# Six of eight output chunks of the down projection: 320 + 320 token columns in place of 384 + 256

## The chip, the cores and the metric

The kernel runs on one core of one Trainium2 chip. The metric is the device time of one execution in microseconds (us); lower is better. Before the change three executions took 981.87, 982.79 and 984.15 us, so the median is 982.79 us.

The engines are named as in the profile: PE is the tensor engine's matrix multiplication, PEld its weight loading, DVE the vector engine, ACT the scalar engine, POOL GpSimd, SP the queue that issues the transfers. Instructions of one engine start in the order in which they were issued to it.

## The reference, cut to what matters

One layer of a diffusion backbone over 512 latent and 128 context tokens, 640 tokens in all, model width 1024. The change touches the last matrix product of the layer, the down projection of the gated feed-forward part, and the two elementwise steps behind it:

```
f_gate, f_val = jnp.split(up, 2, axis=-1)            # up: 640 tokens x 5632
f = (jax.nn.silu(f_gate) * f_val) @ prm["w_ffn_down"]  # (640 x 2816) @ (2816 x 1024)
x = x + g2 * rms_norm(f, prm["norm_ffn_post"])
```

`rms_norm` divides by the root of the mean square over the 1024 channels. Everything is float32 at the edges.

## The kernel before

Activations lie with channels on the 128 partitions and the 640 tokens along the free axis (`T = 640`). A float32 product is made of three products of rounded parts: weights and activations are each split into a high part (rounded to the PE's faster 32-bit format, fp32r) and a low remainder, and `mm3` adds high times high, high times low and low times high in one accumulator in PSUM. A weight block is 128 x 128, and each of the three products of a block is applied to all 640 tokens. One matmul writes at most one PSUM bank of 512 float32 columns, so 640 tokens need two matmuls. They are cut as `HC = ((0, 384), (384, 640))`: a matmul over 384 columns and then one over 256 columns, both with the same weights. Each matmul instruction is preceded by its own weight load, also the second one of a pair.

The cut at 384 has a second use: at several places the two column ranges are worked on one after the other as "halves" 0 and 1, so that elementwise work on one half runs beside matmuls on the other. There a half is a stream of matmuls of one width only.

An accumulator is a PSUM tile of 1024 columns, two banks (`psum`, called `ps` in the profile). `HALF`, inside the kernel function, has the place of each half: 384 columns from column 128 to the bank's end at 512, and 256 columns from 512. The 640 results thus lie next to each other over the border of the banks, and `view` gives them as one range, `t[:, 128:768]`.

The down projection (`down_mm`, `down_out`) makes 8 output chunks of 128 channels, `m` from 0 to 7. Each needs `NF = 22` weight blocks, that is 22 x 3 = 66 pairs of matmuls.

- Chunk 0 uses two single-bank tiles (`zero_at`, called `pq` in the profile) with 384 and 256 columns. It is interleaved with chunk 1: both run over blocks 0 to 15 first, and then over blocks 16 to 21.
- Chunks 1 to 6 use `ps` tiles and pass `half = None`: both column ranges, a pair for each weight.
- Chunk 7 is worked in halves: all 66 matmuls of 384 columns, then the 66 of 256 columns, among which stand the column sums for the norm of half 0.

When a chunk is finished `down_out` reads it from PSUM with ACT: the squares of all 640 columns (L1412, added up by POOL on L1414), then a copy scaled by a per-channel factor, in two parts because latent and context tokens have different factors (L1418). The next chunk takes another of three `ps` tiles meanwhile. Weights come by DMA in units of 8 blocks, and ACT (L311) and POOL (L313) split them into high (`wh`) and low (`wl`) parts ahead of their use.

The order of all instructions on each engine is written out in a table of numbers (`ORDER`); it counts instructions and knows nothing of their widths. In the profile every matmul of `mm3` has line L415. A similar helper on L1259 serves the first part of the up projection.

Of the kernel before, what the change touches and what calls it, by code (L numbers as in the profile page):

```python
# [17 lines left out]
T = L + C  # L18
HT = T // 2
HC = ((0, 384), (384, T))  # L20
NCH = T // P
KD = D // P
NPAIR = 8
# [6 lines left out]
NF = DFF // P  # L30
# [153 lines left out]
def hybrid_layer_kernel(ctx: ExitStack, tc: tile.TileContext, xT, ct, prm, cst, wrest, wdt, idhl_d, wada1, wada2, win,  # L184
# [20 lines left out]
    def nm(s):  # L205
        uid[0] += 1
        return f"{s}_{uid[0]}"


    def slot(tag, dt=F32, shape=(P, T)):  # L210
        if tag in ("H8", "T8"):
            return sb.tile([P, T + 64], dt, tag=tag, name=nm(tag))[:, 48:48 + shape[1]]
        return sb.tile(list(shape), dt, tag=tag, name=nm(tag))
# [4 lines left out]
    def psq(i):  # L218
        return ps.tile([P, 512], F32, tag=f"Q{i}", name=nm(f"pq{i}"))

    def view(t):
        return t[:, 128:128 + T]

    def prm_col(name, i=0, n=1):
        a = _COLS[name][0] + i
        return prms[:, a:a + n]
# [5 lines left out]
    for k in range(KD):  # L232
        t = slot(f"T{k}")
# [58 lines left out]
    def get_unit(i):  # L292
        fetch(i + AHEAD)
        return ready.pop(i)
# [43 lines left out]
    for p in range(NPAIR):  # L338
# [4 lines left out]
        last = p == NPAIR - 1  # L343
# [54 lines left out]
    def split_act(hi_tag, lo_tag, src, lo_eng):  # L398
        hi = slot(hi_tag, F32R)
        hi_ins[0] = ac.activation(hi, src, AF.Copy)  # L400
        lo = slot(lo_tag, F32R)
        split_ins[0] = lo_eng.tensor_tensor(lo, src, hi.bitcast(F32), SUB)
        return hi, lo

    last_mm = [None]
    HALF = ((128, *HC[0]), (512, *HC[1]))

    def mm3(pt, hi, lo, j, xh, xl, first, last, halves=(0, 1), places=None):
        w1 = hi[:, j * P:(j + 1) * P]
        w2 = lo[:, j * P:(j + 1) * P]  # L410
        for i, (w, x) in enumerate(((w1, xl), (w1, xh), (w2, xh)) if first else ((w1, xh), (w1, xl), (w2, xh))):
            for h in halves:
                o, c0, c1 = HALF[h]
                out = places[h] if places else pt[:, o:o + c1 - c0]
                last_mm[0] = te.matmul(out, w, x[:, c0:c1], start=first and i == 0, stop=last and i == 2)  # L415

# [108 lines left out]
    for s in range(4):  # L525
# [6 lines left out]
        for k in (k0, k0 + 1):  # L532
# [3 lines left out]
            hi, lo = split_act(f"H{k}", f"H{8 + k}", xs_[k], ve)  # L536
# [16 lines left out]
    def proj(n):  # L553
        (u,) = unit_of[n]
        hi, lo = get_unit(u)
        pt = psum(flip[0] % 2)
        flip[0] += 1
        for k in range(KD):
            mm3(pt, hi, lo, k, h_hi[k], h_lo[k], k == 0, k == KD - 1)
        return pt  # L560

    def conv3_silu(pt, i, out):
        v = view(pt)
        w = lambda j: prm_col("ssd_w", 3 * i + j)
        ac.activation(out, v, AF.Identity, bias=prm_col("ssd_b", i), scale=w(1))
        for c0, c1 in ((0, L), (L, T)):
            ve.scalar_tensor_tensor(out[:, c0 + 1:c1], v[:, c0:c1 - 1], w(0), out[:, c0 + 1:c1], MUL, ADD)
        for c0, c1 in ((0, L), (L, T)):
            ve.scalar_tensor_tensor(out[:, c0:c1 - 1], v[:, c0 + 1:c1], w(2), out[:, c0:c1 - 1], MUL, ADD)
        if i < NPAIR:  # L570

            tmp = sm.tile([P, T], F32, tag="tanh", name=nm("tanh"), bufs=1)
            ac.activation(tmp, out, AF.Tanh)
            ve.scalar_tensor_tensor(out, tmp, 1.0, out, ADD, MUL)
        else:
            ac.activation(out, out, AF.Silu)
# [7 lines left out]
    def chunked(t):  # L584
        return t.rearrange("p (c t) -> p c t", c=NCH)

# [9 lines left out]
    def dtprep():  # L596
# [5 lines left out]
        pd = psq(0)  # L602
        for c in range(NCH):
            te.matmul(pd[:, c * 32:(c + 1) * 32], raw[:, c * P:(c + 1) * P], ids, start=True, stop=True)
        W = NCH * 32
        scr = slot("T9")
        a, n, e, w = (scr[:, i * W:(i + 1) * W] for i in range(4))
        by = lambda t: t.rearrange("p (c h) -> p c h", c=NCH)
        ve.tensor_tensor(by(a), by(pd[:, 0:W]), prm_col("dt_bias", 0, 32).unsqueeze(1).to_broadcast([P, NCH, 32]), ADD)
        ve.scalar_tensor_tensor(n, a, -1.0, a, MUL, MAX)  # L610
        ac.activation(e, n, AF.Exp, scale=-1.0)

        DT = slot("T12")[:, 0:W].rearrange("p (c h) -> p c h", c=NCH)
        ve.tensor_scalar(n, e, 2.0, None, ADD)
# [235 lines left out]
    def gate(p, pg):  # L850
        for (o0, o1), (c0, c1) in UCOLS:
            ac.activation(ub[p % 3][:, o0:o1], view(pg)[:, c0:c1], AF.Tanh, scale=0.5)

    def gated(p, pa):
        u = ub[p % 3]
        for (o0, o1), (c0, c1) in UCOLS:
            ve.scalar_tensor_tensor(u[:, o0:o1], u[:, o0:o1], 1.0, view(pa)[:, c0:c1], ADD, MUL)
# [69 lines left out]
    for it in seq:  # L927
        if it[0] == "proj":
            n = it[1]
            pt = proj(n)  # L930
# [6 lines left out]
            elif n[0] == "B":  # L937
                g = int(n[1:])
                bT[g] = slot("M2")
                conv3_silu(pt, 8 + g, bT[g])  # L940
            elif n[0] == "C":
                g = int(n[1:])
# [58 lines left out]
    def ahead_parts():  # L1001
        for m in range(KD):
            w = get_unit(unit_of["ahead", m])
            pt = psum(2 if m in (5, 7) else 0)
            for k in range(NA):
                mm3(pt, *w, k, *mix[k], k == 0, k == NA - 1)
            o = ahead_sb[m] = slot(ASLOT[m])
            ac.activation(o, view(pt), AF.Copy)
# [29 lines left out]
    def next_ps():  # L1038
        rot[0] += 1
        return psum(rot[0] % 3)  # L1040

    BOTH = (0, 1)
    RANGES = (((0, *HC[0]),), ((0, HC[1][0], L), (1, L, T)))

    def cols_of(halves):
        return slice(HC[halves[0]][0], HC[halves[-1]][1])

    def ranges_of(halves):
        return ((0, 0, L), (1, L, T)) if len(halves) == 2 else RANGES[halves[0]]
# [49 lines left out]
    def xr_fetch():  # L1099
        for k in range(KD):  # L1100
            t = slot(f"T{8 + k}")
            sy.dma_start(t[:, slice(*HC[0])], xT[:, k, slice(*HC[0])])
            xr[0].append(t[:, slice(*HC[0])])

# [28 lines left out]
    class Mid:  # L1133
        def __init__(self, half):
            self.half, (self.c0, self.c1) = half, HC[half]
            self.n = self.c1 - self.c0
            self.t = {}
# [70 lines left out]
    for half in range(2):  # L1208
        for m in range(OUT_FULL, KD):
            pt = next_ps()  # L1210
# [32 lines left out]
    f_hl = [None] * NF  # L1243
    f_raw = [None] * NF
    for i in range(KD // 2):
        t = sb.tile([P, 2, HC[1][1] - HC[1][0]], F32, tag=f"H{i}", name=nm("xr"))
# [70 lines left out]
    for i in (0, 3, 4, 1, 2):  # L1317
        if i >= 3:
            pt = psq((i + 1) % 2)
# [22 lines left out]
    for i in range(HEAD, 2 * NF):  # L1342
        q, half = ups[i]
        w = get_unit(unit_of["up", i])
        pt = next_ps()
# [48 lines left out]
    def down_mm(m, half, pt, ks):  # L1394
        halves = BOTH if half is None else (half,)
        for k in ks:
            g = k // 8
            if k % 8 == 0 and not half:
                down_w[g] = get_unit(unit_of["down", m, g])
            mm3(pt, *down_w[g], k % 8, *f_hl[k], k == 0, k == NF - 1, halves, zero_at if m == 0 else None)  # L1400

    def down_out(m, half, pt):
        halves = BOTH if half is None else (half,)
        if mg[m] is None:
            mg[m] = slot(mtags[m])
        cc = cols_of(halves)
        v = zero_at[half] if m == 0 else view(pt)[:, cc]
        if m == 0:
            ac.activation(msq[:, cc], v, AF.Square)
        else:  # L1410
            sq = sq_last[0] if half else slot("AT" if m % 2 else "HL")
            ac.activation(sq[:, cc], v, AF.Square)  # L1412
            if half is None:
                gp.tensor_tensor(msq[:, cc], msq[:, cc], sq[:, cc], ADD)  # L1414
            else:
                sq_last[half] = sq
        for c, c0, c1 in ranges_of(halves):
            ac.activation(mg[m][:, c0:c1], v[:, c0 - cc.start:c1 - cc.start], AF.Copy, scale=gg2[:, m, c:c + 1])  # L1418

    down_w = {}  # L1420
# [30 lines left out]
    zero_at = [psq(h)[:, 0:HC[h][1] - HC[h][0]] for h in range(2)]  # L1451
    down_ps = [None, next_ps()]
    for ks in (range(0, 16), range(16, NF)):
        for m in range(2):
            down_mm(m, None, down_ps[m], ks)
            if ks[-1] == NF - 1:
                for half in (BOTH if m == 0 else (None,)):
                    down_out(m, half, down_ps[m])
    for m in range(2, KD - 1):
        pt = next_ps()  # L1460
        down_mm(m, None, pt, range(NF))
        down_out(m, None, pt)

    m = KD - 1
    pt = next_ps()
    down_mm(m, 0, pt, range(NF))
    down_out(m, 0, pt)
    pt = next_ps()
    k1, k2 = 3, 9
# [127 lines left out]
```

## Time and profile before

| | |
|---|---|
| median of the three timed executions | 982.79 us |
| the profiled execution, first to last instruction (its span) | 979.4 us |
| matmuls and weight loads recorded | 7623 each |
| six chunks with pairs in one `ps` tile each (m = 1 to 6) | within about 807 to 946.7 us of the span |
| mean granted tensor clock | 0.996 of full speed |

The profiled execution's own time is told as its span alone; the median of the timed executions is 3.4 us above that span. This is what lies around the first and the last instruction.

A row of the timeline gives the start of a group of like instructions in us from the span's start, the time from there to the end of the last of them, the engine, the line, output and inputs, and how many there are. Matmuls overlap in these records: the next one starts well before the record of the last one ends. What a stream of matmuls costs is therefore read from one start to the next and not from the length of a record.

A row "A <- B: us, times, longest" of the waits says how long engine and line A stood idle until B released it.

### The profile page before, as it was taken

The page shows a single profiled execution, that of the slowest core. Times are in us where ns is not written, and L with a number is a line of the kernel's source. Part 1 is how long each engine was busy: PE and PEld are TensorE (multiplying, and loading weights), DVE is VectorE, ACT ScalarE, POOL GpSimd, SP SyncE. Part 2 cuts the span into 40 slices and gives each one's busy share as a digit, 9 for nine tenths or more (in the row PEclk, how much of TensorE's full clock was granted, in tenths as well). Part 3 has the DMA queues.
Part 4 walks back from the last instruction along what each step waited for, and adds up shares of the span by engine and source line. Part 5 has one row for each costly group of instructions (what it writes and reads, how often), then busy time and mean ns, then how long its engine had stood idle before and what let it go on. Part 6 is the DMA issues. An engine that isn't in the chain of part 4 may idle for free.

```text
span 979.4 us, 18795 instructions
## 1 busy us (share of the span) xinstructions
PE 944.5 (96%) x7623; PEld 920.9 (94%) x7623; DVE 686.9 (70%) x1076; ACT 471.3 (48%) x799; POOL 577.9 (59%) x416
## 2 busy tenths in 40 slices
PE   4999999999999999999999999999999999999995
PEld 3799999999999998998889999999999999999995
DVE  1769898999989997523585998998988898400004
ACT  4355666877668477622464852323232336322211
POOL 1334699889999882534662994444454436543434
PEclk9999999999999999999999999999999999999998
DMA  9622424433424422578662322222222231322213
GB/s 347 250 72 86 117 82 127 146 95 123 139 80 142 128 91 93 196 244 303 200 218 88 129 86 69 84 78 73 86 66 86 66 87 54 94 69 76 82 38 108
DMA packets 50294, 117.52 MB, mean 120 GB/s; under 512 B 6016, under 2 KB 13952, under 8 KB 50208
## 3 DMA queue, kind: packets, MB, share of 16 engines
q1 hardware_dynamic: 50208, 116.33, 37.2%
q8 instruction: 60, 0.98, 0.4%
q14 instruction: 26, 0.21, 0.1%
HBM read 112.55 MB, written 3.75 MB: 119 GB/s over the span
## 4 chain that ended last, share of the span: by engine, by line
PE 87%; DMA 3%; ACT 3%; DVE 2%; SPq 1%; POOL 1%; issue 1%; POOLq 0%; ACTq 0%; DVEq 0%
PE ps L415 72%; PE ps L1259 3%; PE pq L415 2%; PE pq L818 2%; PE pq L807 1%; PE pq L460 1%; SPq L452 1%; DMA wr<-in_wout 1%; PE pq L744 1%; PE pq L441 1%; POOL wl L313 1%; PE pq L473 1%; DMA S<-acD 1%; ACT wh L311 1%; DMA T<-in_wada 1%
## 5 line engine op out<-in xcount | busy, mean ns | idle before, releaser
L313 POOL TENSOR_TENSOR wl<-wr,wh 128x1024 fp32r<-128x1024 f32 (+3 forms) x127 | 290.4, 2290 | 316.3 <-ACT wh L311 299.2
L415 PE MATMUL ps<-H,wh 128*128 128x384 f32 (+1 forms) x1636 | 315.7, 309 | 0.1
L311 ACT ACTIVATE wh<-wr 128x1024 fp32r<-128x1024 f32 (+3 forms) x131 | 131.3, 1003 | 316.2 <-PE ps L415 183.2
L415 PE MATMUL ps<-T,wh 128*128 128x384 f32 (+1 forms) x1472 | 272.5, 306 | 1.8 <-ACT S L1227 1.8
L1237 DVE SCALAR_TENSOR_TENSOR S<-ps,prms,S 128x441 f32<-128x441 f32 (+2 forms) x336 | 233.5, 695 | 29.4 <-ACT S L1227 18.9
L415 PEld LDWEIGHTS ps<-H,wh 128*128 128x128 f32 x1636 | 249.0, 188 | 2.7 <-issue 1.7
L415 PEld LDWEIGHTS ps<-T,wh 128*128 128x128 f32 x1472 | 218.9, 188 | 2.2 <-ACT S L1227 2.1
L872 DVE SCALAR_TENSOR_TENSOR ps<-u,prms,ps 128x655 f32<-128x655 f32 x205 | 185.1, 903 | 10.8 <-ACT ps L869 4.8
L415 PE MATMUL ps<-H,wl 128*128 128x384 f32 (+1 forms) x818 | 191.8, 309 | 0.0
L415 PE MATMUL ps<-T,wl 128*128 128x384 f32 (+1 forms) x736 | 166.2, 305 | 0.0
L415 PEld LDWEIGHTS ps<-H,wl 128*128 128x128 f32 x818 | 129.0, 188 | 1.0 <-issue 1.0
L415 PEld LDWEIGHTS ps<-T,wl 128*128 128x128 f32 x736 | 113.0, 188 | 0.0
L488 DVE RECIPROCAL rsm<-rsm 128x160 f32<-128x160 f32 (+2 forms) x9 | 7.4, 817 | 147.1 <-ACT rsm L487 147.1
L415 PE MATMUL ps<-S,wh 128*128 128x384 f32 (+1 forms) x420 | 88.0, 310 | 1.6 <-ACT wh L311 1.6
L415 PEld LDWEIGHTS ps<-S,wh 128*128 128x128 f32 x420 | 66.5, 188 | 2.8 <-ACT wh L311 1.8
L415 PE MATMUL ps<-S,wl 128*128 128x384 f32 (+1 forms) x210 | 54.9, 309 | 0.3 <-POOL wl L313 0.3
L789 ACT ACTIVATE S<-S,AC 128x128 f32<-128x128 f32 x140 | 45.5, 392 | 2.4 <-DMA S<-acD 2.4
L885 POOL TENSOR_TENSOR T<-T,T 128x640 f32<-128x640 f32 x20 | 32.0, 1602 | 12.5 <-ACT T L881 12.5
L1227 ACT ACTIVATE S<-ps,prms 128x640 f32<-128x640 f32 x42 | 36.5, 869 | 0.0
L415 PEld LDWEIGHTS ps<-S,wl 128*128 128x128 f32 x210 | 35.2, 188 | 0.9 <-POOL wl L313 0.5
L881 ACT ACTIVATE T<-u,prms 128x512 f32<-128x512 f32 (+1 forms) x54 | 27.9, 554 | 6.8 <-POOL T L885 6.8
L1339 POOL TENSOR_TENSOR H<-S,S 128x640 f32<-128x640 f32 x16 | 25.3, 1581 | 0.0
(346 smaller groups left out, 1180.3 us busy)
## 6 DMA issues: line engine op xcount, KB each, us to landing
wr<-in_wup SPq DMA_DIRECT2D x44, 512.0 KB, 3.5
wr<-in_win SPq DMA_DIRECT2D x36, 512.0 KB, 3.9
T<-in_wada SPq DMA_DIRECT2D x49, 256.0 KB, 5.4
S<-acD SPq DMA_DIRECT2D x28, 320.0 KB, 4.7
wr<-in_wdown SPq DMA_DIRECT2D x16, 512.0 KB, 3.4
wr<-in_wout SPq DMA_DIRECT2D x13, 512.0 KB, 4.5
H<-in_wada SPq DMA_DIRECT2D x23, 256.0 KB, 4.6
S<-in_wada SPq DMA_DIRECT2D x16, 256.0 KB, 5.4
```

Source lines behind the costliest of these rows:

```text
L311: ac.activation(hi[:, :n], raw[:, :n], AF.Copy)
L313: lo_eng.tensor_tensor(lo[:, :n], raw[:, :n], hi[:, :n].bitcast(F32), SUB)
L415: last_mm[0] = te.matmul(out, w, x[:, c0:c1], start=first and i == 0, stop=last and i == 2)
L789: ac.activation(rc, rc, AF.Relu, scale=-1.0, bias=AC2[:, c, row:row + 1])
L818: te.matmul(py[64 * h:64 * h + 64, i * P:(i + 1) * P], xt[:, c * P + 64 * h:c * P + 64 * h + 64], rs[h, d][:, c * P:(c + 1) * P], start=d ...
L872: ve.scalar_tensor_tensor(acc, u[:, j:j + UO], w(j), acc, MUL, ADD)
L881: ac.activation(t[:, b:c], u[:, a:a + c - b], AF.Copy, scale=w(j))
L885: gp.tensor_tensor(far, far, t, ADD)
L1227: ac.activation(out, v, AF.Identity, bias=prm_col("ffn_b", i), scale=w(1, 1))
L1237: ve.scalar_tensor_tensor(ob, vl[:, r0 + a - 1:r1 + a - 1, q0 + b - 1:q1 + b - 1], w(a, b), ob, MUL, ADD)
L1259: te.matmul(pt[:, o:o + c1 - c0], w[k] if i in (1, 2) else w[:, k * P:(k + 1) * P], x[:, c0:c1], start=k == 0 and j == 0, stop=k == KD - 1 ...
L1339: gp.tensor_tensor(f_raw[q], a, b, MUL)
```

## The change

In chunks 1 to 6 each pair of matmuls with the same weights covers the 640 tokens as 320 + 320 columns instead of 384 + 256. The two places in the PSUM tile are moved so that the results are again contiguous: 320 columns from 192 to the bank's end at 512, and 320 from 512 to 832. `view` gets a flag that shifts the range which `down_out` reads. Chunk 0 and chunk 7 keep their halves. `HALF` moves to the top of the file.

```
+HALF = ((128, *HC[0]), (512, *HC[1]))
+EVEN = ((512 - T // 2, 0, T // 2), (512, T // 2, T))
...
-    def view(t):
-        return t[:, 128:128 + T]
+    def view(t, even=False):
+        o = EVEN[0][0] if even else HALF[0][0]
+        return t[:, o:o + T]
...
-    HALF = ((128, *HC[0]), (512, *HC[1]))
-
-    def mm3(pt, hi, lo, j, xh, xl, first, last, halves=(0, 1), places=None):
+
+    def mm3(pt, hi, lo, j, xh, xl, first, last, halves=(0, 1), places=None, cuts=HALF):
...
-                o, c0, c1 = HALF[h]
+                o, c0, c1 = cuts[h]
...
-            mm3(pt, *down_w[g], k % 8, *f_hl[k], k == 0, k == NF - 1, halves, zero_at if m == 0 else None)
+            mm3(pt, *down_w[g], k % 8, *f_hl[k], k == 0, k == NF - 1, halves, zero_at if m == 0 else None,
+                EVEN if half is None and m else HALF)
...
-        v = zero_at[half] if m == 0 else view(pt)[:, cc]
+        v = zero_at[half] if m == 0 else view(pt, half is None)[:, cc]
```

What stands on PE in one of the six chunks (m = 5) before the change, a little behind its beginning; `S_670` is the high part of one block's activations, `S_714` and `S_715` are the high and the low part of the next one's, `wh` and `wl` those of the weights, and the last number is the columns streamed:

```order
L415 MATMUL ps_853_10123<-S_670_6459,wl_10025 128x384
L415 MATMUL ps_853_10123<-S_670_6459,wl_10025 128x256
L415 MATMUL ps_853_10123<-S_714_7165,wh_10023 128x384
L415 MATMUL ps_853_10123<-S_714_7165,wh_10023 128x256
L415 MATMUL ps_853_10123<-S_715_7167,wh_10023 128x384
L415 MATMUL ps_853_10123<-S_715_7167,wh_10023 128x256
```

Each weight is used by a 384 and a 256 in turn. The same place on PE after the change, where two like rows print as one with x2 and the line number of `mm3` is two higher:

```order
L417 MATMUL ps_853_10123<-S_670_6459,wl_10025 128x320 x2
L417 MATMUL ps_853_10123<-S_714_7165,wh_10023 128x320 x2
L417 MATMUL ps_853_10123<-S_715_7167,wh_10023 128x320 x2
L417 MATMUL ps_853_10123<-S_714_7165,wl_10025 128x320 x2
L417 MATMUL ps_853_10123<-S_740_7614,wh_10023 128x320 x2
```

Nothing moves. The number and the order of the instructions are the same on PE, and on ACT, DVE, POOL and SP every row is the same as before apart from line numbers. What differs on PE is 396 pairs, 6 chunks x 22 blocks x 3 products.

## The prediction

> **What bounds the kernel now.** I first read the page's busy shares, the granted clock and the chain that ended last.
>
> ```profile
> PE 944.5 (96%) x7623; PEld 920.9 (94%) x7623; DVE 686.9 (70%) x1076; ACT 471.3 (48%) x799; POOL 577.9 (59%) x416
> PEclk9999999999999999999999999999999999999998
> PE 87%; DMA 3%; ACT 3%; DVE 2%; SPq 1%; POOL 1%; issue 1%; POOLq 0%; ACTq 0%; DVEq 0%
> ```
>
> PE is busy throughout and carries 87% of the chain. The clock is granted in full in every slice but the last, so a change in matmul spacing will not be one of clock. A share over the whole span says little about one stage, so next come the stretch in which chunks 2 to 6 run, its waits, and the chain from there to the end.
>
> ```profile
> 847.00:947.00 100.00, 100.00 (x698) 100.00 (x697) 0.00 (x0) 24.72 (x37) 43.53 (x21) 1.00 0.26 76
> POOL wl L313 <- ACT wh L311: 56.0, 16, 4.5
> ACT wh L311 <- PE ps L415: 54.3, 11, 5.8
> 846.87 112.60 PE ps L415 x771
> ```
>
> In these 100 us PE and the weight loads never pause, DVE does nothing, and ACT is busy for 24.7 us. ACT stood 54.3 us waiting for PE to give back weight buffers, and POOL waited for ACT. The weights are therefore ready ahead of PE, and no wait of PE is listed. The last row is one unbroken piece of the chain: 112.6 us of matmuls. Whatever a matmul costs here goes one to one into the time, in either direction.
>
> The change makes no instruction and takes none away, so what decides is how the start-to-start time of a matmul depends on its columns. I look at three streams of the timeline. The first is the alternation of 384 and 256, in chunk 3:
>
> ```profile
> 880.01 0.45 PE L415 MATMUL ps<-T,wl 128*128 128x384 f32 x2
> 880.30 0.73 PE L415 MATMUL ps<-T,wh 128*128 128x384 f32 x4
> ...
> 883.46 0.45 PE L415 MATMUL ps<-H,wl 128*128 128x384 f32 x2
> 883.74 0.45 PE L415 MATMUL ps<-H,wh 128*128 128x384 f32 x2
> ```
>
> (A group is named after its first member, so the 256s hide under "128x384".) Between the first start and the last lie 26 matmuls, x2 and x4 in turn: 3.73 us / 13 pairs = 286.9 ns per pair of 640 columns. The 100 us window agrees: 100 / 698 is 143.3 ns each, or 143.7 if two of the 698 had begun before it, so 286.5 to 287.4 per pair. I use 287.0.
>
> The second and third are streams of one width, in chunk 7, which runs half by half on the same inputs:
>
> ```profile
> 946.84 0.34 PE L415 MATMUL ps<-S,wh 128*128 128x384 f32 x1
> 947.01 0.34 PE L415 MATMUL ps<-S,wl 128*128 128x384 f32 x1
> 947.19 0.52 PE L415 MATMUL ps<-S,wh 128*128 128x384 f32 x2
> ...
> 949.30 0.51 PE L415 MATMUL ps<-T,wh 128*128 128x384 f32 x2
> ```
>
> From 946.84 to 949.30 there are 14 matmuls of 384 columns (x1, x1, x2, x1, and so on): 2.46 / 14 = 175.7 ns each.
>
> ```profile
> 963.34 0.28 PE L415 MATMUL ps<-T,wl 128*128 128x256 f32 x1
> 963.46 0.40 PE L415 MATMUL ps<-T,wh 128*128 128x256 f32 x2
> ...
> 964.78 0.28 PE L415 MATMUL ps<-H,wl 128*128 128x256 f32 x1
> 964.90 0.28 PE L415 MATMUL ps<-H,wh 128*128 128x256 f32 x1
> ```
>
> From 963.34 to 964.90 there are 13 of 256 columns (x1 and x2 in turn): 1.56 / 13 = 120.0 ns each.
>
> This is the finding on which I build. Apart, a 384 and a 256 cost 175.7 + 120.0 = **295.7 ns**; in turn, **287.0**. A matmul that follows one of another width starts the next one earlier than a matmul that follows its like. The lengths of the records say it a second time:
>
> ```profile
> L415 PE MATMUL ps<-S,wh 128*128 128x384 f32 x78 | 24.0, 332 | 0.0
> L415 PE MATMUL ps<-S,wh 128*128 128x256 f32 x76 | 21.2, 279 | 0.0
> L415 PE MATMUL ps<-S,wh 128*128 128x384 f32 x13 | 3.4, 337 | 0.0
> L1259 PE MATMUL ps<-T,H 128*128 128x256 f32 x27 | 3.7, 282 | 0.0
> ```
>
> The first two rows are of the alternation (847 to 947 us), the third is of the 384 stream (947 to 957) and the fourth of a 256 stream in the up projection (530 to 540). A record is some 162 ns longer than the spacing (337 - 175.7 = 161, 282 - 120.0 = 162), so in turn the 384 costs about 332 - 162 = 170 and the 256 about 279 - 162 = 117, 287 in all; apart both are longer.
>
> **The change part by part.**
>
> *The cut.* It touches 6 chunks x 22 blocks x 3 products = 396 pairs. The unknown is the spacing of 320s that follow 320s, and no row has that width. Between the two one-width streams the slope is (175.7 - 120.0) / 128 = 0.435 ns per column, which gives 120.0 + 64 x 0.435 = 147.9 per matmul and 295.7 per pair. Change per pair: 295.7 - 287.0 = +8.7 ns; times 396 = **+3.4 us**.
>
> Low end: the columns alone, without any fixed cost, at that slope: 320 x 0.435 = 139.2, 278.4 per pair, -8.6 x 396 = -3.4 us. High end: from 175.7 down by 64 columns at the flatter slope of the alternation, (170 - 117) / 128 = 0.414: 149.2, 298.4 per pair, +11.4 x 396 = +4.5 us. I take the middle of the one-width streams, because each 320 follows a 320 and those are the nearest rows.
>
> *Both members of a pair use the same weights.* So do two of three neighbours in chunk 7 (`wh`, `wh`, `wl`), and that stream has the 175.7. No term of its own.
>
> *The moved places in PSUM and the shifted range.* The reads by ACT keep their 640, 512 and 128 columns, and as before the 640 and the 512 cross the bank border at column 512. Cost nothing. The cover, if one of them grew, is ACT's idle time, some 75 of the 100 us above, and the three tiles that take turns: a chunk lasts 66 x 287 ns = 18.9 us. For PE to feel it a read would have to last longer by several us.
>
> *Transfers, weight splits, DVE.* They keep their order and their number, and PE asks for weights a little later if it is slower. If it were faster by the low end, 3.4 us in six chunks of 18.9, the 54.3 us of ACT's waiting covers that many times over.
>
> *Behind the chunks.* Chunk 7 and the norm's tail follow PE and are shifted as a whole.
>
> Sum: +3.4 us on the span of 979.4, so 982.8. Around the span lie 3.4 us up to the median of the timed runs, which I leave as they are: 982.8 + 3.4 = **986.2 us**.
>
> **The rivals.**
>
> *The cost is in the columns and in the number of instructions, and history plays no part (no change).* Then 640 columns in two matmuls cost 287.0 however they are cut, and the time stays at 982.8. For it: in all pairs there are two loads and 640 columns. Against it: the one-width streams cost 8.7 ns more for the same two loads and 640 columns, and in the 384 stream neither DVE (0.00 in the window) nor the weights' supply can be to blame. A weaker form is that a pair's second 320 starts like the second of an alternation, since it goes to the other bank. The Trainium skill, "TensorE: Matmul & The Clock Gate", section "Back-to-back issue gap", has this rule as columns / 2.4 + 2.5 ns for an isolated warm matmul; as an estimate, 271.7 ns for either cut, and no change. Here the trace disagrees with the rule in size, 287.0 and 295.7.
>
> *The 256 is held up by its weight load (faster).* Place: the start of each 384 after a 256. The floor shows in the tail:
>
> ```profile
> 962.37 0.88 PE pq L481 x8
> ```
>
> Matmuls of only 96 columns come 0.88 / 8 = 110 ns apart, 10 less than 256 columns do, so something that does not scale with columns takes about 110. If it is the weight load, a 256 has no room for it beside its own streaming, a 384 has 60 ns, and a 320 some 30. A 320 would then cost what a 384 does in the alternation, less 64 columns: 170 - 64 x 0.435 = 142.2, 284.4 per pair, -1.0 us; if the 256 hides a steeper true slope, down to the low end, -3.4 us. I price it in the middle of these two, -2.2 us, 980.6 us. It decides for faster only where a 320 costs less than 143.5 ns. The Trainium skill, same page, section "LDWEIGHTS (loading the stationary operand)", gives columns / 1.2, an estimate of 107 ns for 128 columns; the 110 ns row agrees. Against it: in the 384 stream the load has room to spare, and that stream is the one that loses most against the alternation, 175.7 against 170.
>
> *The change does not do what it says.* The listed order shows 320s in pairs and nothing else moved. I give it no chance.
>
> **How the numbers follow.** A measurement of this kernel can tell some 0.2%, 2.0 us, from no change; per pair that is 5 ns. Forecast, 320s behave as one-width streams do: 0.60. No change: 0.22. Weight load relieved: 0.18. The forecast's own ends by the rows are +2 to +4.5 us, 984.8 to 987.3. The range takes these, the no-change case and the nearer part of the faster case, and 0.7 us for the spread of the timed runs: 980.4 to 988.0. About 0.1 below and under 0.05 above are left out. Faster by over 0.2%: 0.18; within 0.2%: 0.23; slower: 0.59.
>
> **What would show it.** In the changed profile the starts of 320s should lie 147 to 149 ns apart, the records of 320 columns last 309 to 311 ns on average (the average of the alternation is 305.5), and a window of 100 us inside the chunks hold some 676 to 679 matmuls in place of 698. The piece of the chain from about 847 us should grow by 2.9 us, 5 chunks' worth, with PE still without a pause. If the records last 305 or less, the step from one-width streams to 320s is wrong; at 300 the weight load was the cause. If spacing is as forecast and the time is not, something behind the chunks took it up, and the tail after chunk 7 would be shorter.

## The result, and the profile after

The changed kernel took 987.69 us (median of 4 runs, 985.68 to 989.41), the kernel before 982.53 us (4 runs, 981.87 to 984.15). The ratio is 1.0051, with a 95% interval of 1.0033 to 1.0069: slower by 5.2 us, some 3.2 to 6.8 us. A second comparison with more runs (experiment 1) gives 1.0028, 1.0015 to 1.0040, that is +2.8 us. Both say slower, by well under one per cent. How the two sizes go together is the first question below.

The page of the changed kernel: PE still carries the chain, the span is 7.2 us longer, and the clock line now has an 8 in the second slice.

```profile
span 986.6 us, 18795 instructions
PE 950.6 (96%) x7623; PEld 926.9 (94%) x7623; DVE 687.2 (70%) x1076; ACT 471.1 (48%) x799; POOL 576.1 (58%) x416
PEclk9899999999999999999999999999999999999998
PE 87%; DMA 5%; ACT 3%; POOL 2%; DVE 1%; issue 1%; SPq 1%; POOLq 0%; ACTq 0%
```

Then the stretch from the end of chunk 1 to chunk 6, first its busy time (window, busy us and count for PE, weight loads, DVE, ACT and POOL, then the clock), then who waited, then the piece of the chain that begins with the last 18 pairs of chunk 1. (So did the piece of 771 from 846.87 us before the change: chunk 2 itself began at 851.87 us, chunk 7 at 946.67 us. The piece holds those 18 pairs, the 330 of chunks 2 to 6 and the 384s and first 256s of chunk 7.)

```profile
852.00:952.00 100.00, 100.00 (x684) 100.00 (x684) 0.00 (x0) 24.45 (x36) 43.09 (x21) 1.00 0.25 75
```

```profile
POOL wl L316 <- ACT wh L314: 58.9, 16, 4.6
ACT wh L314 <- PE ps L417: 51.2, 10, 6.0
```

```profile
851.98 114.69 PE ps L417 x771
```

The picture is the same as before, at another pace. PE does not pause, ACT and POOL still wait for PE, and 100 us hold 684 matmuls in place of 698. The same 771 matmuls of the chain take 114.69 us in place of 112.60.

The timeline of chunk 3 has the new spacing:

```profile
884.96 0.45 PE L417 MATMUL ps<-T,wl 128*128 128x320 f32 x2
885.25 0.75 PE L417 MATMUL ps<-T,wh 128*128 128x320 f32 x4
...
888.48 0.45 PE L417 MATMUL ps<-H,wl 128*128 128x320 f32 x2
888.77 0.45 PE L417 MATMUL ps<-H,wh 128*128 128x320 f32 x2
```

From 884.96 to 888.77 there are 26 matmuls: 3.81 / 13 = 293.1 ns per pair. Over 640 consecutive starts the trace has 293.2, against 287.2 before: **+6.0 ns per pair**. The records of the 320s, grouped by form, last 308 to 309 ns:

```profile
L417 PE MATMUL ps<-S,wh 128*128 128x320 f32 x152 | 28.4, 309 | 0.0
L417 PE MATMUL ps<-T,wl 128*128 128x320 f32 x80 | 18.2, 308 | 0.0
```

396 pairs x 6.0 ns are 2.4 us, but the span grew by 7.2. Nearly all of the rest arose ahead of the first changed instruction. The first matmuls of chunk 0, which is not changed and runs ahead of everything that is, start here before (the row gives count, shortest, median and longest record, and first and last start):

```profile
L415 PE MATMUL pq<-S,wh x28: 274/306/338, 807.0 to 843.7; 128*128 128x384 f32 x14, 128*128 128x256 f32 x14
```

and here in the changed kernel:

```profile
L417 PE MATMUL pq<-S,wh x28: 274/308/344, 811.7 to 848.7; 128*128 128x384 f32 x14, 128*128 128x256 f32 x14
```

So 4.7 us (4.6 by the exact starts) were lost before the first changed instruction, in code that is the same row for row. From there to the piece of 771 the delay grows to 851.98 - 846.87 = 5.1 us. The other 48 pairs of chunk 1 give 48 x 6.0 ns = 0.3 of it. The remaining 0.2 stand in the last 18 pairs of chunk 0, which are still 384 + 256. Their piece of the chain before the change and after it:

```profile
841.70 5.17 PE pq L415 x36
846.59 5.39 PE pq L417 x36
```

By the starts these unchanged pairs take 287.2 ns before and 299.3 after. Then the piece of 771, with 348 pairs that are changed, adds 114.69 - 112.60 = 2.1. That makes 7.2, and it leaves nothing for the tail.

Where the 4.6 us arose shows when the n-th matmul of both traces is set side by side (counted from 0, starts in us, and by how much the changed kernel is late):

```
n-th matmul   before    after    late
   150         23.30    23.26   -0.04
   300         36.28    38.19   +1.91
  3900        470.80   471.76   +0.96
  4050        487.66   489.97   +2.31
  4500        530.82   533.96   +3.13
  4650        552.64   557.26   +4.62
  6600        825.60   830.22   +4.62
```

The steps to the 300th, the 4050th and the 4650th matmul (1.95, 1.35 and 1.49 us) make 4.8. The others, -0.95 up to the 3900th and +0.82 up to the 4500th, nearly cancel, and no lowered clock goes with them. The three stand where the granted clock (third from the right) was lower than before. Before the change these windows read:

```profile
20.00:40.00 20.00, 17.52 (x272) 13.32 (x275) 16.32 (x36) 5.57 (x9) 6.89 (x3) 1.00 1.02 378
470.00:490.00 20.00, 18.13 (x208) 17.53 (x201) 12.26 (x22) 9.57 (x15) 12.92 (x9) 1.00 0.63 190
540.00:560.00 20.00, 18.24 (x127) 18.06 (x126) 19.06 (x32) 17.76 (x27) 19.84 (x17) 1.00 0.42 139
```

and in the changed kernel's profile:

```profile
20.00:40.00 20.00, 16.65 (x210) 12.36 (x207) 14.43 (x30) 5.57 (x9) 6.47 (x3) 0.83 0.91 339
470.00:490.00 20.00, 17.98 (x197) 17.22 (x196) 12.60 (x20) 8.85 (x15) 12.27 (x8) 0.91 0.58 177
540.00:560.00 20.00, 18.24 (x120) 18.06 (x119) 19.06 (x32) 17.62 (x28) 19.84 (x16) 0.91 0.41 133
```

Losing 0.09 of 20 us, 1.8 us, is what half clock for some 3.6 us would give, and 0.17 twice that. The Trainium skill, "TensorE: Matmul & The Clock Gate", section "What's actually happening", gives half as the low state of the clock and names a window of 3413 ns that runs freely and does not start with the kernel. The clock records of the changed kernel's trace agree with this length: half clock for 6.8 us from 24.0 us on, and for 3.4 us from 484.8 and from 546.2. A pause of PE alone does not decide it: just ahead of the last of these PE stood idle for 1.76 us, and the kernel before had a pause of 1.76 us at the same matmul and kept its clock.

### The profile page after: what moved, and what is told of

Same layout as the page of the kernel before. It is cut to its first block, busy times and chain, and to the rows that moved or that the text cites. A ratio compares the mean times of both kernels' runs of the same rounds, so it can differ in the third digit from the quotient of the medians.

```text
span 986.6 us, 18795 instructions
## 1 busy us (share of the span) xinstructions
PE 950.6 (96%) x7623; PEld 926.9 (94%) x7623; DVE 687.2 (70%) x1076; ACT 471.1 (48%) x799; POOL 576.1 (58%) x416
## 4 chain that ended last, share of the span: by engine, by line
PE 87%; DMA 5%; ACT 3%; POOL 2%; DVE 1%; issue 1%; SPq 1%; POOLq 0%; ACTq 0%
PE ps L417 73%; PE ps L1261 3%; PE pq L417 2%; DMA T<-in_wada 2%; PE pq L820 2%; PE pq L809 1%; PE pq L462 1%; ACT wh L314 1%; PE pq L746 1%; POOL wl L316 1%; DMA S<-acD 1%; DMA wr<-in_wout 1%; PE pq L443 1%; DMA S<-in_wada 1%; PE pq L594 1%
## 5 line engine op out<-in xcount | busy, mean ns | idle before, releaser
L417 PE MATMUL ps<-H,wh 128*128 128x384 f32 (+2 forms) x1636 | 316.5, 309 | 0.1
L417 PE MATMUL ps<-T,wh 128*128 128x384 f32 (+2 forms) x1472 | 274.2, 307 | 1.8 <-ACT S L1229 1.8
L417 PEld LDWEIGHTS ps<-T,wh 128*128 128x128 f32 x1472 | 221.5, 188 | 2.2 <-ACT S L1229 2.1
L874 DVE SCALAR_TENSOR_TENSOR ps<-u,prms,ps 128x655 f32<-128x655 f32 x205 | 185.0, 903 | 11.6 <-ACT ps L871 5.7
L417 PE MATMUL ps<-H,wl 128*128 128x384 f32 (+2 forms) x818 | 191.9, 309 | 0.0
L417 PE MATMUL ps<-T,wl 128*128 128x384 f32 (+2 forms) x736 | 167.1, 307 | 0.0
L417 PE MATMUL ps<-S,wh 128*128 128x320 f32 (+2 forms) x420 | 90.0, 315 | 2.0 <-ACT wh L314 2.0
L417 PEld LDWEIGHTS ps<-S,wh 128*128 128x128 f32 x420 | 69.1, 192 | 3.2 <-ACT wh L314 2.2
L417 PE MATMUL ps<-S,wl 128*128 128x384 f32 (+2 forms) x210 | 55.4, 312 | 0.0
```

The costliest lines, as they stand in the source:

```text
L874: ve.scalar_tensor_tensor(acc, u[:, j:j + UO], w(j), acc, MUL, ADD)
```

## The experiments

Two questions were open. Do the 4.6 us ahead of the chunks belong to the change? And why does 384 + 256 cost less than other cuts: is it that neighbours differ in width, is it a place in memory, or is it these two widths?

**1 and 2: both kernels again, unchanged, five rounds on one chip.**

> The changed kernel once more, beside the kernel before on one chip. In the first comparison it was 5.2 us slower, but its trace has only 2.6 us of the 7.2 us of longer span inside the six chunks; 4.6 us stand ahead of the first changed matmul, in stretches where the granted clock fell to half. Theory A (those 4.6 us are an accident of the clock's windows and have nothing to do with the change): the difference of medians shrinks to +2 to +3 us, and runs of both kernels spread over some 4 us with the granted clock. Theory B (the changed kernel provokes the lower clock ahead of the chunks): +4.5 to +6 us again, with a lower clock than the kernel before in most runs. In the trace: 320s 146 to 147 ns apart, 293 ns per pair.

> The kernel before, unchanged, timed against itself. Theory A: no difference of medians beyond 1 us, single runs spread over 2 to 4 us, and clock windows at half speed at varying places ahead of the chunks. Theory B: clock 0.996 in all runs, spread under 2 us. In the trace 287 ns per pair in chunks 1 to 6.

Measured: the changed kernel 985.18 us (12 runs, 982.85 to 986.77), the kernel before 982.40 us (23 runs, 979.29 to 986.66): ratio 1.0028, 1.0015 to 1.0040, so +1.5 to +3.9 us. The kernel before as an entry of its own took 982.89 us (12 runs, 980.2 to 987.53): ratio 1.0007, 0.9989 to 1.0026, no difference. Clocks ran from 0.993 to 0.997 in the changed kernel's runs and from 0.991 to 0.997 in the 12 runs of the kernel before. The second profile of the kernel *before* has the lowered windows as well:

```profile
20.00:40.00 20.00, 17.21 (x223) 12.64 (x223) 15.01 (x32) 5.70 (x10) 7.12 (x3) 0.91 0.99 364
540.00:560.00 20.00, 18.23 (x118) 18.06 (x117) 19.05 (x32) 16.68 (x27) 19.84 (x17) 0.91 0.43 145
```

This is theory A: the lower clock comes and goes in both kernels, and the comparison shrank to +2.8 us, with the 2.4 us of the chunks inside its interval. The pair spacings repeat exactly, 293.2 and 287.2 ns. The traces also give the change's own cost without what lies ahead of it: from the first matmul of chunk 0 to the end of the span the kernel before takes 172.4 us in both of its traces, the changed one 175.0 and 174.9. That is **+2.6 us**, 2.4 in the changed pairs and 0.2 in the end of chunk 0. One thing was not as expected: the kernel before spread over 7 us, where 2 to 4 had been expected. That the first comparison's excess was an accident of few runs is thus well supported, though of those four runs only one has a trace. By the three steps above the clock is the larger part of it, and it is not all. The code ahead of chunk 0 is the same in all 14 traces of this document, and they reach chunk 0 between 804.5 and 811.7 us: the six without a lowered clock between 20 us and the tail at 804.5 to 807.8, the two with two windows of 3.4 us at 808.7 and 809.7, and the one with four, the first trace of the changed kernel, last of all.

**3, 4, 9 and 10: other cuts.** Only one line differs, here for 352; 400, 376 and 368 are made alike.

```
-EVEN = ((512 - T // 2, 0, T // 2), (512, T // 2, T))
+EVEN = ((512 - 352, 0, 352), (512, 352, T))
```

> The six chunks cut as 352 + 288. Theory 'unlike neighbours' (a matmul that follows one of another width gets on earlier, whatever the difference): 287 ns per pair, as with 384 + 256. Theory 'proportional' (the gain grows with the difference of widths, here half of that of 384 + 256): 290 ns per pair. Theory 'weight load' (the narrower matmul of a pair is what is held up, so nearer to even is never worse): 293 ns or less per pair, with the 288s at or under 128 ns. Inside the chunks that is 0, +1.2 and +2.4 us against the kernel before.

> The six chunks cut as 400 + 240. 'Unlike neighbours': 287 ns per pair. 'Proportional' (difference 160, a quarter more than now): 285 ns, 0.9 us less than the kernel before inside the chunks. 'Weight load' (240 columns have less room than 256, and 110 ns is the floor): the 240s stay at 115 to 118 ns, the 400s take 176 to 177, so 292 to 295 ns per pair, +2 to +3 us.

> The six chunks cut as 376 + 264. Theory 'rhythm' (only the exact pair 384 and 256 in turn falls into a cheap rhythm): 293 ns per pair. Theory 'difference' (the wide one gains when the one before it is narrower by some 100 columns or more and is not yet at the floor of 110 ns): 287 ns.

> The six chunks cut as 368 + 272. 'Rhythm': 293 ns per pair. 'Difference' (96 columns): 287 to 290 ns.

Each kernel of experiments 3 to 12 was timed once, at 981.95 to 987.28 us, which a spread of some 7 us ahead of the chunks makes useless for effects of 3. So their spacings are read. Measured, from 640 consecutive starts of each trace that begin with the last 18 pairs of chunk 1, in ns, and in the last column the us from the first matmul of chunk 0 to the end of the span:

| cut | wide | narrow | pair | chunk 0 to end |
|---|---|---|---|---|
| 384 + 256 (kernel before) | 168.8 | 118.4 | 287.2 | 172.4 |
| 320 + 320 (changed kernel) | 146.6 | 146.6 | 293.2 | 175.0 |
| 352 + 288 | 163.1 | 130.3 | 293.4 | 175.0 |
| 368 + 272 | 170.3 | 125.1 | 295.4 | 175.7 |
| 376 + 264 | 176.2 | 121.6 | 297.8 | 176.7 |
| 400 + 240 | 184.6 | 110.3 | 294.9 | 175.5 |

The windows agree. First the cut of 376, where 607 matmuls stand in 90 us:

```profile
853.00:943.00 90.00, 90.00 (x607) 90.00 (x606) 0.00 (x0) 19.97 (x28) 38.39 (x19) 1.00 0.24 73
```

The kernel before has 629 in the same window:

```profile
853.00:943.00 90.00, 90.00 (x629) 90.00 (x628) 0.00 (x0) 20.80 (x29) 38.86 (x20) 1.00 0.26 76
```

Taking off two matmuls that began earlier, 90 / 605 = 148.8 and 90 / 627 = 143.5 ns. "Unlike neighbours" and "proportional" fall with 352, 376 and 400, where neighbours differ by 64, 112 and 160 columns and nothing is gained. The 376s are the plainest case, since eight columns less than 384 cost 7 ns more. "Weight load" named the pair about right for 352 and for 400 and missed the members: the 288s took 130.3 ns where 128 was its limit, the 400s 184.6 where 176 to 177 was expected. The 240s run at 110.3 ns, the floor, while the 256s stand at 118.4, above it, so a 256 is not held at the floor. "Rhythm", set up for 376 and 368, named 293 for both. It has the side right (no gain) and not the size, 297.8 and 295.4. "Difference" named 287, and 287 to 290, and falls.

**5: the same two widths, 256 first.**

```
+EVEN = ((256, 0, 256), (512, 256, T))
```

> The six chunks cut as 256 + 384: the same two widths in turn, but the 384 reads from byte 1024 of a row and the places in PSUM start at column 256 and at 512. Theory 'widths' (384 and 256 in turn are cheap as such): 287 ns per pair. Theory 'addresses' (cheap is a place in the row or in PSUM that is a multiple of 512 bytes together with the widths): also 287, since all of these still are. If it is 293 or more, it was the order or the offset 1536 of the second operand.

Measured: 287.2 ns per pair (384s 168.9, 256s 118.3). The order and the places do not matter.

```profile
853.00:943.00 90.00, 90.00 (x628) 90.00 (x628) 0.00 (x0) 21.21 (x30) 38.72 (x20) 1.00 0.26 77
```

**6, 7 and 8: the same widths, other addresses.** In turn: the operand of the 256s moved, the first 320 moved in PSUM (with ACT's reads adapted in `down_out`), the operand of the second 320 moved.

```
+EVEN = ((128, 0, 384), (512, 320, 576))
...
+EVEN = ((128, 0, 320), (512, 320, T))
+        two = lambda t: t.rearrange("p (h c) -> p h c", h=2)
+        v = zero_at[half] if m == 0 else two(pt[:, 128:896]) if even else view(pt)[:, cc]
...
+EVEN = ((192, 0, 320), (512, 256, 576))
```

> 384 + 256 as before, but the second matmul of each pair in the six chunks reads columns 320 to 576 in place of 384 to 640 (so the result differs): only the offset of its operand changes, from 1536 to 1280 bytes. 'Widths': 287 ns per pair. 'Addresses', where the operand's offset counts: 290 to 294.

> 320 + 320 with the first result at PSUM column 128 in place of 192, so that both start at a multiple of 512 bytes; the reads take the two pieces of 320 (half of each piece gets the factor of the other kind of token, so the result differs). 'Widths': 293 ns per pair as in the changed kernel. 'Addresses', where the place in PSUM counts: 287.

> 320 + 320 placed in PSUM as in the changed kernel, but the second matmul reads columns 256 to 576 in place of 320 to 640 (so the result differs): the operand starts at byte 1024 in place of 1280. 'Widths': 293 ns per pair. 'Addresses', where the operand's offset counts: 287.

Measured: 287.2, 293.2 and 293.2 ns per pair. Neither the operand's offset in its row nor the place in PSUM plays a part in these kernels, which compute something else where their operands or reads differ and are read for their spacing alone. The window of the kernel with the moved PSUM place has the changed kernel's count, 616:

```profile
853.00:943.00 90.00, 90.00 (x616) 90.00 (x615) 0.00 (x0) 20.94 (x30) 38.66 (x20) 1.00 0.26 77
```

**11 and 12: one of the two widths changed by 16 columns.**

```
+EVEN = ((128, 0, 384), (512, 368, T))
...
+EVEN = ((112, 0, 400), (512, 384, T))
```

> 384 + 272 in the six chunks: the second matmul of a pair starts 16 columns earlier and overlaps the first (so the result differs by a shift of 16 tokens); 656 columns are streamed per pair. 'Rhythm': the 384 loses its advantage, 175 to 176 ns, and the 272 takes 124 to 126: 300 ns per pair. 'Difference': 384 at 169, 272 at 124 to 126: 294 ns.

> 400 + 256 in the six chunks: the first matmul of a pair streams 16 columns more than before, over which the second writes again (so the result differs by a shift of 16 tokens). 'Rhythm': 400 at 182 to 184 as with 240, 256 at 118: 301 ns per pair. 'Difference': 400 at 176, 256 at 118: 294 ns.

Measured: 384 + 272 gives 176.4 + 123.8 = 300.2 ns, and 400 + 256 gives 185.0 + 119.0 = 304.0. The 384 beside a 272 is back at the cost that it has among its own kind (175.7 in chunk 7). The records grouped by form, first of 384 + 272, then of the swapped kernel of experiment 5, show it on the page:

```profile
L417 PE MATMUL ps<-S,wh 128*128 128x384 f32 x58 | 18.5, 339 | 0.0
L417 PE MATMUL ps<-S,wh 128*128 128x272 f32 x58 | 16.7, 287 | 0.0
```

```profile
L417 PE MATMUL ps<-S,wh 128*128 128x384 f32 x65 | 20.1, 332 | 0.0
L417 PE MATMUL ps<-S,wh 128*128 128x256 f32 x65 | 18.1, 279 | 0.0
```

The same 384 lasts 339 beside a 272 and 332 beside a 256. "Difference" had named 294 for both kernels and falls. Of the mixtures tried, only 384 and 256 in turn ran below 293 ns on average in the chunks, which is what the theory "rhythm" says. The 400 + 256 was 3 ns worse than it named.

But the widths do not decide alone. The 304.0 of 400 + 256 is a mean of two spacings, each of which holds over many pairs. In its trace the first and the last two of these rows are 20 and 24 pairs apart:

```profile
887.45 0.76 PE L417 MATMUL ps<-S,wh 128*128 128x400 f32 x4
...
893.45 0.46 PE L417 MATMUL ps<-S,wl 128*128 128x400 f32 x2
...
897.08 0.47 PE L417 MATMUL ps<-T,wl 128*128 128x400 f32 x2
...
904.44 0.47 PE L417 MATMUL ps<-H,wl 128*128 128x400 f32 x2
```

6.00 us / 20 is 300.0 ns, and 7.36 us / 24 is 306.7. Nor is it the input: the first 13 pairs of chunk 2 are 307 ns apart, those of chunks 3 to 6, with the same activations, 300. The alternation of 384 and 256 has two spacings as well. The last 18 pairs of chunk 0 are the same in every kernel here, and only the cut of the chunk 1 pairs ahead of them differs. They take 287 to 288 ns behind 384 + 256 in either order, 368 + 272 and 400 + 240, and 299 to 300 ns behind 320 + 320, 352 + 288, 376 + 264, 384 + 272 and 400 + 256. The kernel before has the second spacing too, 300 ns from 203.6 to 208.7 us, until two 384s follow each other and 287 begins. So the spacing depends on what ran before as well, and no run here shows how.

No cut that was tried beat the one of the kernel before; 448 + 192 and 512 + 128 were not tried.

## Why the prediction was right, point by point

- **PE sets the end, and spacing goes one to one into the time.** Right. The chain has the same 771 matmuls in one piece, 2.1 us longer, and ACT and POOL wait for PE as before. The tail was shifted as a whole: 4.6 us ahead of the first changed instruction, 0.5 up to the piece and 2.1 in it are all of the 7.2.
- **320s behave as a stream of one width.** Right, and this carried the sign. Forecast 147.9 ns each, measured 146.6; records 309 to 311 forecast, 308 to 309 found. The straight line between the two one-width streams was 1.3 ns too high per matmul. About half of that is the 256 row: its 13 starts gave 120.0 ns, while all 60 that follow one another in chunk 7 give 118.8, by which the line is at 147.2 and the sum at +2.9 us. So a pair lost 6.0 ns and not 8.7, and the chunks 2.4 us and not 3.4: the term of the sum was mis-sized by 1.0 us, about a third. For the same reason the 100 us window held 684 matmuls and not 676 to 679, and the chain's piece grew by 2.1 us and not 2.9. The 0.2 us in chunk 0, whose pairs keep their widths, are in no term of the sum.
- **The reason given, that a matmul following one of another width gets the next one started earlier.** Wrong as a rule. It was read from rows that held only 384 and 256. Experiments 3, 4, 9 and 10 put unlike neighbours next to each other and found the prices of like ones. Among the cuts tried the advantage is that of 384 and 256 alone, and even they lose it in some stretches (299 ns at the end of chunk 0). The forecast survived because 320 + 320 lacks that pair just as it lacks unlike neighbours; in this the sign was partly luck.
- **Moved places in PSUM, at no cost.** Right: experiment 7 moves the place of the 320s, and experiment 5 the places of 256 and 384, without any change of spacing.
- **The rival of no change** fell with 293.2 against 287.2, and its weaker form (the second 320 goes to the other bank, so it should count as alternation) with it.
- **The rival of the weight load** needed 320s below 143.5 ns; they took 146.6. The floor that it spoke of is there, but a 256 is not on it.
- **The time.** Forecast 986.2 us, +3.4. The first comparison gave +5.2 (3.2 to 6.8), the second +2.8 (1.5 to 3.9), and the traces +2.6 from chunk 0 on, 2.4 of it in the changed pairs. That the first median, 987.69, still lay inside the range, 0.3 us below its upper end, was luck as well, since 4.6 of the 7.2 us in its trace arose ahead of the change. The first one's excess stands ahead of the chunks, where the clock differed. The forecast had allowed 0.7 us for the spread of runs, from three runs that agreed within 2.3 us; with more runs the kernel before spread over 7 us. That allowance was the weakest number of the prediction. The 3.4 us taken to lie around the span are some 2 in the executions whose time and span stand side by side (988.76 and 986.6, for one); the rest is presumably the difference between two executions, and it does not touch the forecast of +3.4.

## What to carry to other kernels

Take the cost of a new matmul width from start-to-start times of streams in the trace, and keep apart the widths and the company in which each was seen: here the same 384 columns cost 168.8 or 175.7 ns, and the same pair 287 or 299. An existing cut can sit on a narrow optimum, so an even split that looks better balanced should be measured against the sum of its neighbours and not assumed better. When a change touches one stage, set the two traces side by side at the first changed instruction: a difference that is already there is not the change's.

## What the runs showed of the hardware that had not been expected

In chunks 2 to 6, 384 and 256 columns in turn cost 287.2 ns per pair in every placement and order tried (experiments 5 and 6, and both traces of the kernel before). Every other cut of 640 columns that was tried cost 293.2 to 297.8. Changing either width by 16 columns (experiments 11 and 12) took the advantage away: 300.2 and 304.0 for 656 columns. A line through the one-width streams, 118.8 at 256 and 175.7 at 384, gives 294.5 per pair; the other cuts lie within 3.3 ns of it, the exact pair 7 below. The advantage is almost wholly in the 384 (168.8 in place of 175.7).

That is not a fixed price of these widths: the same alternation took 299 to 300 ns in other stretches, and 400 + 256 changed between 300.0 and 306.7 within one trace, with what had run before. What makes it so inside the engine was not found. Operand offset, PSUM place and order are excluded by the runs for the spacing in the chunks. Whether the rhythm hangs on the time that a weight load takes was not varied here, since every load has 128 columns.

The other surprise is the spread: the lowest and the highest of 35 runs of the unchanged kernel in one session lie 8.2 us apart (979.29 and 987.53), three times the effect that was to be measured.
